# A hybrid mixer's hand-written task order: the second half of the frequencies directly behind the first, first scores between the projection's last steps

## The chip, the cores and the metric

The kernel runs on one core of one Trainium2 chip. Time is device time in microseconds of one launch. The kernel before takes 2418.3 us (median of 3 runs, 2416.39 to 2420.72). All arithmetic is fp32; for the large products an operand is split into a high and a low fp32r part and three products are summed.

## The reference, cut to what matters

Two layers run on 640 tokens (512 latent, 128 context) of width 1024. Each layer is a SwiGLU block, a mixer and a second SwiGLU block, each with modulation by a condition vector. The change lies in the mixer, whose three head groups work on one projection of the same normed input:

```
def mixer(h):                       # per layer, h: 640 x 1024
    u = h @ w_in                    # q, k, v (attention); p (pooling); v0 v1 xa xb xc xd (Hyena)
    pool = group_linear(window_mean(p, 2 | 4 | 8 | 16) - p) * scale
    attn = softmax over |i-j| <= 128 local keys, context keys and a sink (8 heads, 2 kv heads)
    z = (v0, v1)
    for x in ((xa, xb), (xc, xd)):  # Hyena of order 2
        z = short_conv(x) * (long_conv(z) + bias * z)
    return concat(pool, attn, z) @ w_out
```

The long convolution is a transform to frequencies, a product with the filter's spectrum, and the inverse transform, all written as matrix products with tables.

## The kernel before

Channels lie on partitions, tokens on the free axis (640 columns, in two halves of 320). A projection column group of 128 channels is 48 matmuls of 128x320 (8 input channel groups, 3 products of split parts, 2 halves); their PSUM is copied by ScalarE to a tile `u`. The weights come by DMA as `raw`, ScalarE casts them to `whi` (line 294) and VectorE forms `wlo` (line 295).

The mixer's parts are Python generators that issue instructions up to their next `yield`. A string of letters, `MIXP` (line 32), says which generator takes its next step. After it the kernel is compiled by a scheduler which keeps each engine's queue in an order close to this issue order; each engine then works its queue off in order. What follows from the string is thus the order within each queue, and which buffers (rotating slots) are taken over from whom.

The letters that matter here:

- `F` is one step of the projection stream: 12 matmuls, a quarter of the 48 of a column group. The groups come in the order q0 to q3, xa, xb, v, p0, p1, xc, xd; then the output projection's steps. A letter that needs a group which isn't made yet pulls the stream until it is.
- `C` is one step of Hyena (`conv_step_old`, lines 1063 to 1144), for each of its two orders: the transposes `ztp`; the first half of the frequencies (`zf`, then on VectorE `zp`, `zm`, the products `cw`, `cy`, and their sums `pp`, `pmn`); the second half and the context part (`zfc`, `zcs`), with the loads of the four inverse tables `tab` from `in_tfi`; the inverse transform (`yt`, `ytc`); the gate (the short convolution of xc and xd, `sc` with lines 1148 to 1152, the products `yu`, `yw`).
- `P` is the pooling, `pool_mix`: for each of two channel groups the window sums `pw` and the difference `pd` (lines 1171 to 1185, on VectorE, from ScalarE's copies `pl`, `pc`), then in a second step each one's product `pm` and its split `phi`, `plo`.
- `A` is attention: first five steps for head pair 0 (four blocks of scores, each six matmuls `mm<-khi,qhi` and so on and two reductions of line 1398; then the exponentials on ScalarE and the scaling), then the transposes `pt` and products of one pair with the next pair's scores.
- `X` is the context's attention (`sc<-qkc`, `p`), `V` the transposes `vt` of the values, `Q` the queries.

In the stretch that the change re-orders (the second Hyena order), before, the steps come as: first frequency half; pooling group 0; two steps of xc; second frequency half; pooling group 1; inverse transform; the rest of xc; scores block 0; values; block 1; context; block 2; xd, with block 3 and the softmax; the gate (the scheduler takes a block of scores ahead of the inverse transform where it is ready first); the transposes of the probabilities; the output projection.

Of the kernel before, what the change touches and what calls it, by code (L numbers as in the profile page):

```python
# [28 lines left out]
RCP = 300  # L29
RCP2 = 0  # L30
ORDER = "v0 v1 k q0 q1 q2 q3 xa xb v p0 p1 xc xd".split()
MIXP = "FCFFCFFFFFFCFNFCFKFFFFCQQFCQFFQFCPFFCPCFFAVAXAFAAFFCAPFXFAAPFAFFFAFFAAAFAAFFAAFAAAAXFAXFXAFFFFAFABFFBAABBFABAAFAAFFFFFFFF"
PROT = 8
AG0 = (1, 0, 2)
MIXT = 70
# [147 lines left out]
def hybrid_kernel(ctx: ExitStack, tc: tile.TileContext, a, depth=2, fc=22):  # L183
# [974 lines left out]
    def mixer(l, cur, nxt):  # L1158
# [390 lines left out]
        def step(t):  # L1549
            next(tasks[t], None)  # L1550

        for t in MIXP.replace(" ", ""):
            step(t)
# [253 lines left out]
```

## Time and profile before

| | us |
|---|---|
| median of 3 runs | 2418.3 |
| profiled execution | 2417.21 |
| its span in the trace | 2415.4 |
| TensorE busy in the span | 2369.8 (98%) |
| VectorE busy | 1920.3 (80%) |
| ScalarE busy | 1094.6 (45%) |
| mean granted TensorE clock | 0.99 |

The profile is of one execution, and has the durations of all instructions. PE is TensorE, DVE VectorE, ACT ScalarE, SP SyncE, which issues the DMAs. Of a row `out<-in` names the tiles; fp32 matmuls may stand as two records. The time in brackets is the idle time ahead of an instruction, and `<-` what it waited for. The granted clock (PEclk) is 1.00 at the higher of TensorE's two levels and 0.50 at the lower.

### The profile page before, as it was taken

Reading aid. Unit: us, or ns where it says so; the run is one execution under the profiler, and the core shown is the slowest. Engines: PE = TensorE matmul, PEld = TensorE weight load, DVE = VectorE, ACT = ScalarE, POOL = GpSimd, SP = SyncE. Lnnn points to the kernel's source line nnn. Section 1 sums busy time; section 2 is a strip of 40 time slices with the busy share of each in tenths; the row PEclk is TensorE's granted clock in tenths of the full one; section 3 lists DMA queues with packets and bytes.
Section 4 is the critical chain, followed back from the end, with each engine's and each line's share of the span. In section 5 each row is a group of like instructions: output and inputs, shape, how many; then the busy total and the mean of one; then the engine's idle time right before and its main releaser. Section 6 shows DMA issues by size and latency. Waiting matters only on the chain.

```text
span 2415.4 us, 41068 instructions
## 1 busy us (share of the span) xinstructions
PE 2369.8 (98%) x15576; PEld 2246.0 (93%) x15576; DVE 1920.3 (80%) x3885; ACT 1094.6 (45%) x2228; POOL 17.8 (1%) x46
## 2 busy tenths in 40 slices
PE   8999999999989999999999999999998999999999
PEld 3799999999877999999999999999987789999999
DVE  7887888986786798888889889898678678567583
ACT  4653352534345653443535435253434555335251
POOL 0000000000000000000000000000000000000000
PEclk9999999999989999999999999999998999999999
DMA  9434434353210235434343443534231022222222
GB/s 323 168 105 132 134 115 154 101 170 114 102 45 15 78 106 161 127 121 144 117 131 106 124 130 116 164 113 154 89 105 61 18 71 79 79 84 78 85 68 90
DMA packets 132646, 270.37 MB, mean 112 GB/s; under 512 B 15002, under 2 KB 24924, under 8 KB 132320
## 3 DMA queue, kind: packets, MB, share of 16 engines
q1 hardware_dynamic: 132448, 267.75, 34.5%
q8 instruction: 122, 2.00, 0.3%
q14 instruction: 76, 0.62, 0.1%
HBM read 259.56 MB, written 8.13 MB: 111 GB/s over the span
## 4 chain that ended last, share of the span: by engine, by line
PE 93%; DVE 4%; issue 1%; ACT 1%; DMA 1%; SPq 0%; POOL 0%; POOLq 0%; DVEq 0%; ACTq 0%
PE mm L204 79%; PE Z L204 5%; PE yt L204 1%; PE o L204 1%; PE pt L208 1%; PE fk L204 1%; PE mx L204 1%; PE ada L204 1%; PE zf L204 1%; PE rsb L204 0%; PE qbc L204 0%; DMA ar<-in_ada 0%; PE tot L204 0%; DMA par<-in_par 0%; PE nps L204 0%
## 5 line engine op out<-in xcount | busy, mean ns | idle before, releaser
L204 PE MATMUL mm<-hhi,whi 128*128 128x320 f32 x1440 | 448.2, 311 | 1.1 <-ACT u L1220 1.1
L204 PE MATMUL mm<-hlo,whi 128*128 128x320 f32 x1440 | 445.7, 309 | 0.0
L294 ACT CAST whi<-raw 128x512 fp32r<-128x512 f32 (+1 forms) x394 | 238.8, 607 | 456.2 <-PE mm L204 425.9
L204 PE MATMUL mm<-hhi,wlo 128*128 128x320 f32 x1440 | 445.4, 309 | 0.0
L204 PE MATMUL mm<-ahi,whi 128*128 128x320 f32 x1198 | 370.2, 309 | 0.0
L204 PE MATMUL mm<-alo,whi 128*128 128x320 f32 x1198 | 370.2, 309 | 0.0
L204 PE MATMUL mm<-ahi,wlo 128*128 128x320 f32 x1198 | 370.2, 309 | 0.0
L295 DVE TENSOR_TENSOR wlo<-raw,whi 128x512 fp32r<-128x512 f32 (+1 forms) x394 | 262.9, 670 | 77.4 <-ACT whi L294 75.2
L409 DVE CUSTOM_DVE_ANT_0 junk<-araw,condb,par 128x1024 bf16<-128x1024 f32 x240 | 307.1, 1280 | 2.2 <-DMA araw<-in_adat 0.7
L204 PEld LDWEIGHTS mm<-hhi,whi 128*128 128x128 f32 x1440 | 270.3, 188 | 6.0 <-ACT u L1220 2.8
L204 PEld LDWEIGHTS mm<-hlo,whi 128*128 128x128 f32 x1440 | 270.6, 188 | 2.0 <-issue 1.8
L204 PEld LDWEIGHTS mm<-hhi,wlo 128*128 128x128 f32 x1440 | 270.3, 188 | 1.4 <-issue 1.4
L204 PE MATMUL mm<-thi,whi 128*128 128x320 f32 x864 | 267.0, 309 | 0.0
L204 PE MATMUL mm<-tlo,whi 128*128 128x320 f32 x864 | 267.0, 309 | 0.0
L204 PE MATMUL mm<-thi,wlo 128*128 128x320 f32 x864 | 267.0, 309 | 0.0
L204 PEld LDWEIGHTS mm<-ahi,whi 128*128 128x128 f32 x1198 | 224.9, 188 | 0.0
L204 PEld LDWEIGHTS mm<-ahi,wlo 128*128 128x128 f32 x1198 | 224.9, 188 | 0.0
L204 PEld LDWEIGHTS mm<-alo,whi 128*128 128x128 f32 x1198 | 224.9, 188 | 0.0
L294 ACT CAST whi<-ex 128x512 fp32r<-128x512 f32 x216 | 134.2, 621 | 186.9 <-PE mm L204 173.3
L295 DVE TENSOR_TENSOR wlo<-ex,whi 128x512 fp32r<-128x512 f32 x216 | 148.9, 689 | 31.7 <-ACT whi L294 27.2
L294 ACT CAST whi<-ws 128x512 fp32r<-128x512 f32 x144 | 89.4, 621 | 162.2 <-PE mm L204 123.1
L204 PEld LDWEIGHTS mm<-tlo,whi 128*128 128x128 f32 x864 | 162.2, 188 | 0.0
(263 smaller groups left out, 4713.6 us busy)
## 6 DMA issues: line engine op xcount, KB each, us to landing
araw<-in_adat SPq DMA_DIRECT2D x120, 512.0 KB, 3.6
raw<-in_wgu SPq DMA_DIRECT2D x208, 256.0 KB, 3.0
ex<-in_wgu SPq DMA_DIRECT2D x144, 256.0 KB, 2.7
raw<-in_wd SPq DMA_DIRECT2D x128, 256.0 KB, 2.7
raw<-in_win SPq DMA_DIRECT2D x56, 256.0 KB, 2.8
ar<-in_ada SPq DMA_DIRECT2D x48, 256.0 KB, 5.4
raw<-in_wd SPq DMA_DIRECT2D x64, 192.0 KB, 2.6
tab<-in_tfi SPq DMA_DIRECT2D x32, 256.0 KB, 4.1
```

The costliest lines, as they stand in the source:

```text
L204: cls.order(nc.tensor.matmul(**k))
L208: cls.order(nc.tensor.transpose(**k))
L294: S.copy(out=hi, in_=src)
L295: V.tensor_tensor(out=lo, in0=src, in1=hi.bitcast(F32), op=ALU.subtract)
L409: V.tensor_tensor_reduce(out=junk, in0=raw, in1=condb[:, r], scale=1.0, scalar=bias(l, g)[:, s, c, r:r + 1], op0=ALU.mult, op1=ALU.add, ac ...
```

## The change

Only the string `MIXP` is edited; it serves both layers.

```diff
--- before.py
+++ after.py
@@ -29,7 +29,7 @@
 RCP = 300
 RCP2 = 0
 ORDER = "v0 v1 k q0 q1 q2 q3 xa xb v p0 p1 xc xd".split()
-MIXP = "FCFFCFFFFFFCFNFCFKFFFFCQQFCQFFQFCPFFCPCFFAVAXAFAAFFCAPFXFAAPFAFFFAFFAAAFAAFFAAFAAAAXFAXFXAFFFFAFABFFBAABBFABAAFAAFFFFFFFF"
+MIXP = "FCFFCFFFFFFCFNFCFKFFFFCQQFCQFFQFCCPFAFAPAFCAVFAXFFCFAPFXFAAPFAFFFAFFAAAFAAFFAAFAAAAXFAXFXAFFFFAFABFFBAABBFABAAFAAFFFFFFFF"
 PROT = 8
 AG0 = (1, 0, 2)
 MIXT = 70
```

By the steps' names, after the change they come as: first frequency half; second half with the context part; pooling group 0 (with it the projection of p0 and p1); xc step 0; scores block 0; xc step 1; block 1; pooling group 1; block 2; xc step 2; inverse transform; block 3; values; xc step 3; softmax of head pair 0; context; two steps of xd; the gate (with the last two steps of xd); the pooling's products and the first step of the output projection; then transposes and the next pair's scores.

VectorE in layer 0, from the first half's sums `pp`, `pmn` on. Before, a weight split and pooling group 0 (`pw`, `pd`) stand there, and the second half's `zp` inside them:

```order
L1104 TENSOR_TENSOR pp_7300<-cy_7289,cy_7297 128x256 x2
L1105 TENSOR_TENSOR pmn_7301<-cy_7289,cy_7297 128x256 x2
L295 TENSOR_TENSOR wlo_7802<-raw_7799,whi_7801 128x512
L1171 TENSOR_TENSOR pw_7442<-pl_7436 128x527
L295 TENSOR_TENSOR wlo_7914<-raw_7911,whi_7913 128x512
L1181 TENSOR_TENSOR pw_7444<-pw_7442 64x525
L1184 TENSOR_TENSOR pw_7444<-pw_7444,cst 128x8 x2
L1185 SCALAR_TENSOR_TENSOR pd_7438<-pw_7444,cst,u_7368 128x512
L1171 TENSOR_TENSOR pw_7453<-pc_7437 128x143
L295 TENSOR_TENSOR wlo_8023<-raw_8020,whi_8022 128x512
L1181 TENSOR_TENSOR pw_7455<-pw_7453 64x141
L1098 TENSOR_TENSOR zp_7505<-zod_7503,zf_7493 128x512
```

After:

```order
L1104 TENSOR_TENSOR pp_7300<-cy_7289,cy_7297 128x256 x2
L1105 TENSOR_TENSOR pmn_7301<-cy_7289,cy_7297 128x256 x2
L1098 TENSOR_TENSOR zp_7318<-zod_7316,zf_7306 128x512
L1099 SCALAR_TENSOR_TENSOR zm_7319<-zod_7316,zf_7306 128x512
L966 TENSOR_TENSOR cw_7322<-zp_7318,kf_7157 128x512
L968 TENSOR_TENSOR cw_7323<-zp_7318,kf_7157 128x256 x2
L970 TENSOR_TENSOR cy_7327<-cw_7322 128x256
L971 TENSOR_TENSOR cy_7327<-cw_7323 128x256
L966 TENSOR_TENSOR cw_7330<-zm_7319,kf_7159 128x512
L968 TENSOR_TENSOR cw_7331<-zm_7319,kf_7159 128x256 x2
```

The second half's sums and products stand directly behind the first half's; the splits and the pooling have moved behind them.

TensorE in layer 0, at the inverse transform. Before, all of it (`yt`) stands behind the first block of scores (`mm<-khi,qhi`):

```order
L204 MATMUL mm_7650<-klo_6961,qhi_7097 128x384
L204 MATMUL mm_7651<-klo_6961,qhi_7097 128x384
L204 MATMUL mm_7650<-khi_6960,qlo_7098 128x384
L204 MATMUL mm_7651<-khi_6960,qlo_7098 128x384
L204 MATMUL yt_7585<-tab_7531,pp_7300 128x256
L204 MATMUL yt_7585<-tab_7533,pp_7300 128x256
L204 MATMUL yt_7585<-tab_7535,pp_7525 128x256
L204 MATMUL yt_7585<-tab_7537,pp_7525 128x256
L204 MATMUL yt_7585<-tab_7531,pmn_7301 128x256
L204 MATMUL yt_7585<-tab_7533,pmn_7301 128x256
L204 MATMUL yt_7585<-tab_7535,pmn_7526 128x256
L204 MATMUL yt_7585<-tab_7537,pmn_7526 128x256
```

After, the first three `yt` stand at the end of p1's matmuls, ahead of xc (`mm<-hhi,whi`, first of 48) and of all scores; the fourth and the rest stand behind another 54 rows, with three blocks of scores among them:

```order
L204 MATMUL mm_7431<-hhi_6109,wlo_7465 128x320
L204 MATMUL mm_7431<-hhi_6113,whi_7464 128x320
L204 MATMUL mm_7431<-hlo_6114,whi_7464 128x320
L204 MATMUL mm_7431<-hhi_6113,wlo_7465 128x320
L204 MATMUL yt_7641<-tab_7344,pp_7300 128x256
L204 MATMUL yt_7641<-tab_7346,pp_7300 128x256
L204 MATMUL yt_7641<-tab_7348,pp_7338 128x256
L204 MATMUL mm_7520<-hhi_6075,whi_7524 128x320
L204 MATMUL mm_7520<-hlo_6076,whi_7524 128x320
L204 MATMUL mm_7520<-hhi_6075,wlo_7525 128x320
```

The tables are now needed ahead of xc, and the inverse transform is spread over the projection.

VectorE in layer 0 again, with the engines that each instruction waits for, where pooling group 1 begins (`pw<-pl` of 128x527). Before, it stands behind the context's products and waits for ScalarE and GpSimd:

```order
L968 TENSOR_TENSOR cw_7545<-zcs_7542,kf_7160 128x256 [waits DVE_49]
L968 TENSOR_TENSOR cw_7545<-zcs_7542,kf_7160 128x256
L970 TENSOR_TENSOR cy_7549<-cw_7544 128x256 [waits DVE_49]
L971 TENSOR_TENSOR cy_7549<-cw_7545 128x256 [waits DVE_49]
L1171 TENSOR_TENSOR pw_7558<-pl_7552 128x527 [waits Activation_49,Pool_49]
L1181 TENSOR_TENSOR pw_7560<-pw_7558 128x525 [waits DVE_49]
L1181 TENSOR_TENSOR pw_7562<-pw_7560 128x521 [waits DVE_49]
L1181 TENSOR_TENSOR pw_7564<-pw_7562 64x513 [waits DVE_49]
L1184 TENSOR_TENSOR pw_7564<-pw_7564,cst 128x8 [waits DVE_49,Activation_49]
```

After, it stands behind the reductions of scores block 1 (line 1398, ISA):

```order
L1185 SCALAR_TENSOR_TENSOR pd_7497<-pw_7514,cst,u_7427 128x128 [waits DVE_49]
L295 TENSOR_TENSOR wlo_7975<-raw_7972,whi_7974 128x512 [waits DMAHW4_49,PE_49,Activation_49]
L1398 ISA sc_7574,m_7540<-mm_7566,m_6928,par_190 128x512 [waits DVE_49,PE_49]
L1398 ISA m_7540 128x1
L1398 ISA sc_7576,m_7541<-mm_7567,m_6928,par_190 128x512 [waits PE_49]
L1398 ISA m_7541 128x1
L1171 TENSOR_TENSOR pw_7584<-pl_7578 128x527 [waits PE_49,Activation_49,Pool_49]
L1181 TENSOR_TENSOR pw_7586<-pw_7584 128x525 [waits DMAHW1_49,DVE_49,PE_49]
L1181 TENSOR_TENSOR pw_7588<-pw_7586 128x521 [waits DVE_49]
L1181 TENSOR_TENSOR pw_7590<-pw_7588 64x513 [waits DVE_49,PE_49]
L1184 TENSOR_TENSOR pw_7590<-pw_7590,cst 128x8 [waits DVE_49,Activation_49]
L1184 TENSOR_TENSOR pw_7590<-pw_7590,cst 128x8
```

Its place is behind two blocks of scores, and its first instructions now wait for TensorE as well.

## Rows read from the trace of the kernel before

**Rows 1.** The page: busy time, share of the span and instructions of each engine.

```profile
PE 2369.8 (98%) x15576; PEld 2246.0 (93%) x15576; DVE 1920.3 (80%) x3885; ACT 1094.6 (45%) x2228; POOL 17.8 (1%) x46
```

**Rows 2.** TensorE's waits: releaser, total, times, longest (us).

```profile
PE pt L208 <- DVE sc L1353: 7.6, 4, 3.6
...
PE yt L204 <- DMA tab<-in_tfi: 3.5, 2, 3.1
```

**Rows 3.** TensorE's timeline, layer 0: start, us, instruction; in brackets idle time and releaser.

```profile
662.23 0.42 PE L204 MATMUL mm<-hhi,whi 128*128 128x320 f32 x1 [0.57 <-ACT u L1220]
...
677.82 0.34 PE L204 MATMUL mm<-khi,qlo 64*128 64x384 f32 x2
...
681.21 2.04 PE L204 MATMUL yt<-tab,pp 128*128 128x256 f32 x4 [3.05 <-DMA tab<-in_tfi]
...
683.72 2.04 PE L204 MATMUL yt<-tab,pp 128*128 128x256 f32 x4 [0.46 <-DMA tab<-in_tfi]
...
688.50 1.89 PE L204 MATMUL yt<-tab,pp 128*128 128x256 f32 x8
...
690.23 1.89 PE L204 MATMUL yt<-tab,pmn 128*128 128x256 f32 x8
...
709.86 0.78 PE L208 MATMUL pt<-ident,sc 128*128 128x128 f32 x2 [3.58 <-DVE sc L1353]
...
717.31 0.41 PE L204 MATMUL mm<-plo,whi 128*128 128x320 f32 x1
...
731.25 0.31 PE L204 MATMUL mm<-yhi,wlo 128*128 128x320 f32 x1
...
731.40 0.31 PE L204 MATMUL mm<-phi,whi 128*128 128x320 f32 x1
```

**Rows 4.** TensorE's timeline, layer 1: the same two points.

```profile
1817.35 0.42 PE L204 MATMUL mm<-hhi,whi 128*128 128x320 f32 x1 [0.57 <-ACT u L1220]
...
1887.94 0.31 PE L204 MATMUL mm<-phi,whi 128*128 128x320 f32 x1
```

**Rows 5.** Busy time by stretch: us, PE, PEld, DVE, ACT, POOL, PEclk, DMA share, GB/s.

```profile
680.00:690.00 10.00, 8.33 (x27) 6.56 (x28) 9.49 (x24) 2.34 (x6) 0.28 (x4) 0.66 0.42 124
...
706.00:718.00 12.00, 8.35 (x30) 5.58 (x30) 10.94 (x24) 7.67 (x17) 0.00 (x0) 0.72 0.06 22
```

**Rows 6.** VectorE's timeline, layer 0.

```profile
663.03 0.69 DVE L1098 TENSOR_TENSOR zp<-zod,zf 128x512 f32<-128x512 f32 x1 [0.45 <-ACT zod L1096]
...
669.46 0.68 DVE L295 TENSOR_TENSOR wlo<-raw,whi 128x512 fp32r<-128x512 f32 x1
...
675.09 0.69 DVE L1098 TENSOR_TENSOR zp<-zod,zf 128x512 f32<-128x512 f32 x1
...
681.27 0.76 DVE L1105 TENSOR_TENSOR pmn<-cy,cy 128x256 f32<-128x256 f32 x2
...
681.94 0.69 DVE L295 TENSOR_TENSOR wlo<-raw,whi 128x512 fp32r<-128x512 f32 x1
...
684.65 0.71 DVE L1171 TENSOR_TENSOR pw<-pl 128x527 f32<-128x527 f32 x1
...
690.58 0.61 DVE L1398 CUSTOM_DVE_ANT_0 sc<-mm,m,par 128x384 f32<-128x384 f32 x1
```

**Rows 7.** SyncE's queue, layer 0: the four table loads.

```profile
678.48 2.37 SPq L260 DMA_DIRECT2D tab<-in_tfi  x4
```

**Rows 8.** ScalarE's timeline, layer 0.

```profile
701.19 0.62 ACT L1349 ACTIVATE sc<-sc,sm 128x384 f32<-128x384 f32 x1 [1.62 <-DVE sm L1347]
...
704.68 0.43 ACT L1220 COPY u<-mm 128x320 f32<-128x320 f32 x1 [0.27 <-PE mm L204]
...
707.53 0.19 ACT L1349 ACTIVATION_READ_ACCUMULATOR sc<-sc,sm 128x1 f32 x1
```

**Rows 9.** VectorE's timeline, layer 0, behind the softmax.

```profile
708.66 0.72 DVE L1150 SCALAR_TENSOR_TENSOR sc<-u,par,sc 128x511 f32<-128x511 f32 x1
...
718.13 1.00 DVE L1196 SCALAR_TENSOR_TENSOR plo<-pm,par,phi 128x320 fp32r<-128x320 f32 x2
```

## The prediction

> **What bounds the kernel now.** I read the busy shares first: TensorE is busy 98% of the span, VectorE 80% [rows 1], so a new order can pay only where TensorE stands still, and any stretch in which it newly stands still costs its full length. Next I read the table of waits: TensorE's largest wait is for the softmax's scaled probabilities (`pt` behind `sc`), and with it goes the inverse transform's wait for its tables (`yt` behind `tab`) [rows 2]. Both lie in the stretch that the change re-orders. Last I read TensorE's timeline there. In layer 0 it runs from the first matmul of projection p1 behind the forward transform (662.23) to the first matmul of the second output group (731.40), 69.17 us; in layer 1 from 1817.35 to 1887.94, 70.59 us [rows 3, 4]. Program order shows the same 307 TensorE instructions between these two points before and after, in both layers, so the change is the difference in these two stretches.
>
> What TensorE could win there: in layer 0 it waits 3.05 and 0.46 us for tables and 3.58 us for the softmax [rows 3]; besides, its clock stands at the lower level for part of 680 to 690 and of 706 to 718 (mean granted 0.66 and 0.72), each time after it had begun to idle [rows 5]. Summing spacings by kind (0.15 us a 320-column matmul, 0.43 us a 256-column fp32 one, half of the distance 1.73 between 688.50 and 690.23 over two such, and so on [rows 3]) I get about 53.3 us at full clock, so at most 69.2 - 53.3 = 15.9 us are to be won in layer 0 and about 17.3 in layer 1.
>
> **What the change moves.** It adds and removes no arithmetic. It does four things: (1) the second frequency half's products go on VectorE directly behind the first half's; (2) the pooling's first channel group goes behind them, the second one behind two blocks of scores; (3) the first head pair's scores go on TensorE between the last projection steps, ahead of the inverse transform's later parts; (4) the gate's inputs xc and xd, and so their copies on ScalarE, come behind the exponentials.
>
> **Step 1, tables and inverse transform.** VectorE's first half begins at 663.03 and is gap-free up to the weight split at 669.46 [rows 6]. Before, the second half began at 675.09; now it follows at 669.46, 5.63 us earlier, and its last product ends near 669.46 + 6.44 = 675.9 (675.09 to the end of `pmn` at 681.94, less 0.41 us of pooling between). The four table loads wait for this half's first products: before they were issued 678.48 - 675.09 = 3.39 us behind its start [rows 6, 7]; now 2.98, at 672.4. The first `yt` started 2.73 us behind the issue [rows 3, 7], so now at 675.2. But TensorE has less to do until then: 48 matmuls of p1 (7.1 us) and two small fp32 products (0.87) end near 670.2. It waits 5.0 us instead of 3.5: 1.5 us lost. Three `yt`, with the third table as late as before (2.5 us behind the first), end near 677.5; then projection xc and scores block 0 follow.
>
> **Step 2, the wait that is new.** VectorE now does, behind 675.9: two weight splits (1.2), the context's products (2.0), pooling group 0 (3.4), one split (0.6), four score reductions (2 x 0.55 and 2 x 0.68); it ends near 686. Scores block 2 on TensorE needs the score buffers that the reductions of block 1 free, so TensorE stands still again from about 682.5 to 686. Behind it stand, in the same queue, three scores' pairs (0.65), six projection matmuls (0.88), nine `yt` (9 x 0.43) and `ytc` (0.44): 5.9 us, to about 692. The first instruction of pooling group 1 (`pw` from `pl`) now waits for the fourth `yt` matmul of the second channel half, since its output takes over a buffer that this matmul reads, and its next instructions for the `yt` behind it; before it waited for no TensorE work and ran at 684.65 [rows 6]. So VectorE stands still from about 686 to 692, and queued behind the waiting `pw` are the reductions of score blocks 2 and 3 and with them the whole softmax. This is the term on which the forecast rests. No row of before shows this wait; its bounds are 0 (if the buffer comes free in time) and 6.8 us (a lower-clock stretch of TensorE on top); I take 6, from the queue's own sum.
>
> **Step 3, softmax, gate, output.** From 692.1: pooling group 1 takes 690.58 - 684.65 = 5.93 us [rows 6], a split 0.6, reductions of blocks 2 and 3 1.5 and 1.25, small copies 1.2: exponentials begin near 702.6; before they began at 701.19 [rows 8]. Before, ScalarE had copied xd between the exponentials of the two heads (704.68) and the last ended at 707.62 [rows 8]. Now both heads (2 x 2.7), their sinks (0.45), two weight casts (1.1), the context's exponentials (1.4) and the short convolution's scaling (0.8) stand in one row, to about 711.8. Then VectorE does the gate's 17 instructions, 7.6 us by the durations behind 708.66, two `ylo` (1.5) and the `plo`, of which the third ends near 722.5. Before, the `plo` ran partly ahead of `ylo`, and the corresponding output matmul started at 717.31 [rows 3, 9]. TensorE has done its other work by about 711 and stands still until about 721: 9 to 10 us, where before it had 3.58.
>
> **Sum.** From 717.31 to 731.40 TensorE needed 14.1 us [rows 3]. After 722.5 there is the same work and 2.65 us more (six scores and seven transposes of the next head that stood earlier before), and about 1 us at the lower clock: 722.5 + 14.1 + 2.65 + 1 = 740.2, that is +8.8 us in layer 0. Layer 1 repeats the stretch 1155.12 us later; 740.2 + 1155.12 = 1895.3 against 1887.94 [rows 4], +7.4. Together +16 us. The profiled execution took 2417.2, 1.1 below the median of the runs; on the median 2418.3 + 16 = **2434 us**.
>
> **Bounds of the unknown terms.** The table loads: the third `yt` waited to 683.72 [rows 3]; if all tables land as that one, step 1 costs 2 us more a layer. The clock: in rows 5 a mean of 0.66 over 10 us is 6.8 us at the lower level, half speed; if it falls so at each of the three new stops and half of that meets work, I estimate up to 3 us more a layer; if it does not fall, 1 us less. The new wait of VectorE: with 0 in place of 6 the mean of both layers, +8.1, falls to +2.1. So a layer lies between about +2.1 and +13.
>
> **Rivals.**
> A (forecast): VectorE's pooling waits for the inverse transform, softmax and gate come late; +16.
> B: as A, and late tables and the lower clock cost 2 and 3 us a layer more: 2418.3 + 16 + 10 = 2444 us. For it: each stop in rows 5 has such a stretch. Against it: two of the three new stops hide part of theirs in the next stop.
> C, the other side: the order does what its names say. Scores and softmax run under the projection, and the inverse transform starts earlier and leaves the path. It decides at one point: the third `plo` has to be done by 713.6, that is 731.40 - 14.1 - 2.65 - 1; before that the kernel is faster, by what it stays below. For it: the scores stand ahead of the projection's last steps, and the tables are issued 6 us earlier. Against it: the waiting `pw` in front of the softmax. Its price: at the 53.3 us limit plus about 7 of waits for tables, 722.5, -8.9 a layer, 2400 us.
> The Trainium skill has a rule for this, "Perfetto Trace Analysis", section "Optimization Strategy": where the most contended engine changes over time, interleaving the regimes may pay. By it scores between projection steps should fill TensorE's waits; the trace bears the rule's premise out (VectorE and ScalarE are the late engines at 701 to 718, TensorE elsewhere), and by it alone the result would be C.
> D: the earlier tables and the new waits cancel, or the new wait of VectorE is short: 0 to +2.4 a layer, 2418 to 2423.
>
> **How the numbers follow.** Chances: A 0.65, B 0.13, C 0.12, D 0.10. A alone is 2426 to 2440. The range leaves out most of C and the top of B: 2420 to 2444. A measurement of this kernel tells 0.2%, 4.8 us, from no change. Slower by more than that: A, B and a little of D, 0.81. Within it: most of D and the edge of C, 0.09. Faster: 0.10.
>
> **What would show it.** Right: TensorE's first `yt` waits near 5 us for `tab`; VectorE idles about 6 us ahead of a `pw` (line 1171) released by TensorE's `yt`; TensorE idles 8 to 10 us ahead of the first output matmul on `phi` or `plo`, near 711 to 721; the first exponentials of the scores begin no earlier than 701. Wrong: that `pw` starts without a wait, exponentials begin by 696, or the second output group's matmul starts below 731.40 in layer 0.

## The result, and the profile after

The changed kernel takes 2451.1 us (median of 4 runs, 2447.21 to 2454.85) against 2419.5 of the kernel before on the same chip: ratio 1.0132, 95% interval 1.0109 to 1.0154, so **31.6 us slower**. The direction was forecast, the size was not: 2434 was said, and the time lies above the range's 2444. The profiled execution took 2448.4 us, its span 2446.6.

The page's first line, of the kernel after [rows 1 of before]:

```profile
PE 2377.1 (97%) x15576; PEld 2252.3 (92%) x15576; DVE 1922.4 (79%) x3885; ACT 1095.3 (45%) x2228; POOL 18.0 (1%) x46
```

The work is the same; the span is longer by 31.2 us, and TensorE's busy time by 7.3. So TensorE stands still longer, and part of what it does takes longer. Where both lie, a table by stretch shows (us, then the busy time of PE, PEld, DVE, ACT, POOL, the granted clock, DMA). First before, from the first matmul of p1 to the second output group's first matmul, in layers 0 and 1 [rows 3, 4]:

```profile
662.23:731.40 69.17, 62.00 (x346) 50.64 (x346) 59.05 (x161) 33.05 (x87) 0.56 (x8) 0.90 0.15 47
1817.35:1887.94 70.59, 62.62 (x346) 50.89 (x346) 59.15 (x161) 33.20 (x87) 0.63 (x8) 0.90 0.14 46
```

The same two points after:

```profile
662.27:747.52 85.25, 67.59 (x345) 55.13 (x346) 59.90 (x159) 33.19 (x85) 0.56 (x8) 0.82 0.11 38
1833.54:1918.33 84.79, 67.40 (x345) 54.69 (x345) 59.92 (x159) 33.19 (x85) 0.56 (x8) 0.84 0.12 37
```

This is nearly the whole account. The stretch is 16.1 us longer in layer 0 and 14.2 in layer 1. In layer 0 idle time grew from 7.2 to 17.7 us (+10.5), and the same instructions (of the 346 records one is missing after) were busy 67.6 instead of 62.0 us (+5.6), because more of them ran at the lower clock; in layer 1 it is +9.4 and +4.8. All the rest of the span is 0.9 us longer.

What TensorE waited for, after (total, times, longest) [rows 2 of before]:

```profile
PE mm L204 <- ACT phi L1195: 17.9, 2, 9.0
PE yt L204 <- DMA tab<-in_tfi: 9.0, 2, 4.5
PE mm L204 <- DVE m L1398: 7.1, 4, 3.5
```

The softmax's `pt` is gone from the top; in its place the first output matmul waits 9.0 us a layer for the pooling's `phi`, and a block of scores 3.5 us for its buffer. TensorE's timeline in layer 0, after [rows 3]:

```profile
662.27 0.42 PE L204 MATMUL mm<-hhi,whi 128*128 128x320 f32 x1 [0.56 <-ACT u L1220]
...
674.95 2.04 PE L204 MATMUL yt<-tab,pp 128*128 128x256 f32 x4 [4.51 <-DMA tab<-in_tfi]
...
700.63 0.69 PE L204 MATMUL mm<-khi,qhi 64*128 64x384 f32 x1 [3.46 <-DVE m L1398]
...
727.27 0.63 PE L204 MATMUL mm<-phi,whi 128*128 128x320 f32 x1 [8.97 <-ACT phi L1195]
...
747.52 0.42 PE L204 MATMUL mm<-phi,whi 128*128 128x320 f32 x1
```

Three stops, each with a stretch at the lower level behind or inside it; the granted clock is the last number but two (1.00 is the higher of TensorE's two levels) [rows 5 of before]:

```profile
670.00:680.00 10.00, 5.13 (x17) 3.85 (x17) 9.86 (x24) 3.24 (x7) 0.14 (x2) 0.66 0.44 157
...
700.00:710.00 10.00, 9.37 (x32) 7.62 (x33) 6.62 (x25) 6.10 (x17) 0.00 (x0) 0.50 0.09 29
...
720.00:730.00 10.00, 2.73 (x8) 2.08 (x9) 9.39 (x17) 3.13 (x6) 0.00 (x0) 0.52 0.00 0
730.00:740.00 10.00, 10.00 (x58) 8.90 (x58) 4.48 (x13) 3.01 (x11) 0.00 (x0) 0.80 0.09 28
```

From 700 to 710 TensorE is almost fully busy, at half speed throughout: that is where most busy time is lost. VectorE's rows of after [rows 6]:

```profile
669.50 0.68 DVE L1098 TENSOR_TENSOR zp<-zod,zf 128x512 f32<-128x512 f32 x1
...
685.95 0.08 DVE L1398 DVE_READ_ACCUMULATOR2_ANT m<- 128x1 f32 x1
693.38 0.71 DVE L1171 TENSOR_TENSOR pw<-pl 128x527 f32<-128x527 f32 x1 [7.35 <-PE yt L204]
```

The forecast wait is there, in the row forecast: pooling group 1 stands 7.35 us behind the inverse transform. ScalarE's rows of after [rows 8]:

```profile
692.42 0.62 ACT L1168 COPY pl<-u 128x512 f32<-128x512 f32 x1 [8.46 <-PE yt L204]
...
705.54 0.61 ACT L1349 ACTIVATE sc<-sc,sm 128x384 f32<-128x384 f32 x1 [1.95 <-DVE sm L1347]
...
711.89 0.62 ACT L294 CAST whi<-raw 128x512 fp32r<-128x512 f32 x1 [3.35 <-PE mm L204]
712.42 0.61 ACT L1349 ACTIVATE sc<-sc,sm 128x384 f32<-128x384 f32 x1
...
726.06 0.72 ACT L294 CAST yhi<-yw 128x640 fp32r<-128x640 f32 x1 [0.93 <-DVE yw L1141]
726.69 1.78 ACT L1195 ACTIVATE phi<-pm,par 128x320 fp32r<-128x320 f32 x4
```

Here is what was not forecast. The copy `pl`, which `pw` reads, waits for a `yt` matmul too, 8.46 us, and ends at 693.04, only 0.34 us before `pw` starts: the pooling's wait stands in two queues. The second head's exponentials start at 712.42, behind a weight cast that waits 3.35 us until TensorE's matmuls (at the lower clock) free its buffer. And `phi`, whose input `pm` was done by 718.3, stands behind both casts of the gate's output `yhi`.

### The profile page after: what moved, and what is told of

Same layout as the page of the kernel before. It is cut to its first block, busy times and chain, and to the rows that moved or that the text cites. A ratio compares the mean times of both kernels' runs of the same rounds, so it can differ in the third digit from the quotient of the medians.

```text
span 2446.6 us, 41080 instructions
## 1 busy us (share of the span) xinstructions
PE 2377.1 (97%) x15576; PEld 2252.3 (92%) x15576; DVE 1922.4 (79%) x3885; ACT 1095.3 (45%) x2228; POOL 18.0 (1%) x46
## 5 line engine op out<-in xcount | busy, mean ns | idle before, releaser
L204 PEld LDWEIGHTS mm<-thi,wlo 128*128 128x128 f32 x864 | 162.2, 188 | 0.0
L204 PEld LDWEIGHTS mm<-thi,whi 128*128 128x128 f32 x864 | 162.2, 188 | 0.0
```

The costliest lines, as they stand in the source:

```text
L204: cls.order(nc.tensor.matmul(**k))
```

## The experiments

Only the piece of `MIXP` behind the common start `...FFQFC` is edited unless said otherwise. The piece of the kernel before is `PFFCPCFFAVAXAFAAFFC APFX...`, of the changed kernel `CPFAFAPAFCAVFAXFFCF APFX...`. Ratios are to the kernel before on the same chip, with 95% intervals; "us" is the ratio less one, times 2418.3, which puts the change itself at +31.9. Theory T: the scores ahead of pooling and softmax make the loss. Rival R: the early frequencies and their wait for tables make it.

| run | median us | ratio (interval) | us |
|---|---|---|---|
| e1_freq | 2419.1 | 1.0001 (0.9990 to 1.0013) | +0.2 |
| e2_scores | 2446.0 | 1.0118 (1.0103 to 1.0134) | +28.5 |
| e3_pool | 2430.4 | 1.0060 (1.0036 to 1.0083) | +14.5 |
| e4_back | 2435.1 | 1.0073 (1.0058 to 1.0088) | +17.7 |
| e5_cast | 2445.7 | 1.0109 (1.0095 to 1.0124) | +26.4 |
| e6_pm | 2442.2 | 1.0102 (1.0086 to 1.0118) | +24.7 |
| e7_near | 2426.1 | 1.0033 (1.0021 to 1.0045) | +8.0 |
| e8_far | 2422.2 | 1.0014 (1.0004 to 1.0024) | +3.4 |
| f1_fill_tab | 2450.5 | 1.0126 (1.0113 to 1.0140) | +30.5 |
| f2_fill_both | 2440.4 | 1.0096 (1.0080 to 1.0113) | +23.2 |
| f3_before_fill | 2416.5 | 0.9981 (0.9970 to 0.9993) | -4.6 |
| f4_before_fill2 | 2418.7 | 0.9996 (0.9985 to 1.0008) | -1.0 |
| h1_all | 2420.4 | 1.0007 (0.9996 to 1.0018) | +1.7 |
| h2_all_fill | 2417.9 | 0.9999 (0.9989 to 1.0009) | -0.2 |
| h3_freq_fill | 2414.4 | 0.9984 (0.9973 to 0.9995) | -3.9 |

**The two halves of the change.**

```diff
 e1_freq, against the kernel before
-PFFCPCFFAVAXAFAAFFC
+CPFFPCFFAVAXAFAAFFC
 e2_scores, against the changed kernel
-CPFAFAPAFCAVFAXFFCF
+PFFCAFAPACAVFAXFFCF
```

> The kernel before with one step of the order moved: the second half of the frequencies directly behind the first; pooling and scores stay as before. Theory T (the loss comes from pooling group 1 and the softmax standing behind the inverse transform): TensorE waits about 5 us for the tables instead of 3.5, scores keep their place, so 0 to +4 us on the kernel before. Rival R (the early frequency half and the wait for tables with the low clock behind it make the loss): +12 to +30 us.

> The other part alone: the second half of the frequencies stays two projection steps behind pooling group 0 as before; scores block 0 and 1 stand between the projection's steps, pooling group 1 behind them and the rest as in the changed kernel. Theory T: most of the loss, +22 to +34 us on the kernel before, with VectorE again idle ahead of pooling group 1 or TensorE idle 8 us or more ahead of the first output matmul. Rival R: under +10 us.

The frequency half alone costs nothing that can be told, the other half (the early scores, with pooling group 1 behind them) nearly everything; R falls. Yet e1_freq has the longer wait for tables, in its table of waits:

```profile
PE yt L204 <- DMA tab<-in_tfi: 9.5, 3, 4.4
PE pt L208 <- DVE sc L1353: 7.2, 4, 3.4
```

The tables' wait is 2.7 times that of before [rows 2], 6 us more, and most of that comes back: the two stretches of this trace are 70.49 and 71.41 us, 2.1 us more than before together. The wait for the softmax behind it stays (7.2 against 7.6 us), which suggests that the softmax ends last there in both kernels.

**Pooling group 1 ahead of its wait.** Two ways, against the changed kernel:

```diff
 e3_pool
-CPFAFAPAFCAVFAXFFCF
+CPPFAFAAFCAVFAXFFCF
 e4_back
-CPFAFAPAFCAVFAXFFCF
+CPCFAFAPAFAVFAXFFCF
```

> The changed kernel with one letter moved: pooling group 1 directly behind group 0, ahead of the scores; the program then has no wait of its first instruction for TensorE. Theory T: VectorE's 7 us of idle time ahead of it go, the first exponentials come some 5 to 7 us earlier, and of the +32 us about 10 to 18 go: +13 to +22 us on the kernel before. Rival R: the tables are as late and the inverse transform as split as in the changed kernel: +26 to +34 us.

> The changed kernel with the inverse transform's step ahead of the first scores, so that it is not split by scores and projection steps and pooling group 1, where it stays, finds its buffers free. Theory T: VectorE doesn't wait for TensorE there, exponentials 4 to 6 us earlier: +14 to +24 us on the kernel before. Rival R in the form that the split of the inverse transform is what costs: 0 to +8 us.

Both times came as T said, and R's versions of both failed. In e3_pool the group runs without the wait (VectorE, ScalarE, TensorE):

```profile
680.87 0.70 DVE L1171 TENSOR_TENSOR pw<-pl 128x527 f32<-128x527 f32 x1
```

```profile
696.72 0.62 ACT L1349 ACTIVATE sc<-sc,sm 128x384 f32<-128x384 f32 x1
...
714.77 1.77 ACT L1195 ACTIVATE phi<-pm,par 128x320 fp32r<-128x320 f32 x4
```

```profile
715.34 0.64 PE L204 MATMUL mm<-phi,whi 128*128 128x320 f32 x1 [8.51 <-ACT phi L1195]
```

The stretch begins at 660.07 in this execution, at 662.27 in the changed kernel's. Counted from there, the first exponentials start 6.6 us earlier than in the changed kernel and 2.3 us earlier than before the change [rows 3, 8], and still the kernel is 14.5 us slower than before: it waits 8.5 us for `phi`. So about 17 us (12 to 23 by the interval of this run's ratio) were the pooling's wait, and the rest lies behind the softmax.

In e4_back the exponentials start 3.1 us earlier, counted in the same way, less than the 4 to 6 expected. The wait ahead of `pw` is gone, but VectorE now waits for TensorE at the first scores instead:

```profile
688.18 0.62 DVE L1398 CUSTOM_DVE_ANT_0 sc<-mm,m,par 128x384 f32<-128x384 f32 x1 [5.07 <-PE mm L204]
```

**The cast and the pooling's products.** Against the changed kernel:

```diff
 e5_cast
-CPFAFAPAFCAVFAXFFCF APFXFAAPF...
+CPFAFAPAFCAVAFXFFCF APFXFAAPF...
 e6_pm
-CPFAFAPAFCAVFAXFFCF APFXFAAPF...
+CPFAFAPAFCAVFAXFFPPCF AFXFAAF...
```

> The changed kernel with one letter moved: the softmax step of the first head pair one projection step earlier, so that on ScalarE a weight cast, which waits for TensorE to free its buffer, stands behind the second head's exponentials instead of ahead of them. Theory: that cast held the exponentials back by 3.4 us a layer, which the prediction had priced at the cast's own 0.6; moved, 3 to 8 us go of the change's +32 (about 2443 to 2448 us). Rival: the chain behind is held by something else (pooling, gate), and nothing goes: 2449 to 2453.

> The changed kernel with the pooling's products pm, phi and plo asked for ahead of the gate instead of behind it. Theory: the first output matmul then waits for the gate's yhi and ylo alone, the 9.0 us of waiting for phi become 2 to 5 us for yhi, and of the +32 us 4 to 9 go (2442 to 2447). Rival: the gate is what ends last, the output matmul waits as long for yhi, 2449 to 2453.

Both as the theories had it: 5.5 and 7.2 us go. In e5_cast the cast that waits for TensorE has moved behind the second head (ScalarE):

```profile
704.72 0.61 ACT L1349 ACTIVATE sc<-sc,sm 128x384 f32<-128x384 f32 x1 [0.72 <-DVE sm L1347]
...
709.99 0.61 ACT L1349 ACTIVATE sc<-sc,sm 128x384 f32<-128x384 f32 x1
711.52 0.62 ACT L294 CAST whi<-raw 128x512 fp32r<-128x512 f32 x1 [0.73 <-PE mm L204]
```

In e6_pm the wait of 9.0 us for `phi` is one of 2.8 for `yhi` (TensorE):

```profile
723.42 0.63 PE L204 MATMUL mm<-yhi,whi 128*128 128x320 f32 x2 [2.83 <-ACT yhi L294]
725.05 0.63 PE L204 MATMUL mm<-ylo,whi 128*128 128x320 f32 x1 [1.01 <-DVE ylo L295]
```

**The three moves together.**

```diff
 h1_all, against the changed kernel
-CPFAFAPAFCAVFAXFFCF APFXFAAPF...
+CPPFAFAAFCAVAFXFFPPCF AFXFAAF...
```

> The changed kernel with the three moves of the runs before together: pooling group 1 ahead of the scores, the first softmax one projection step earlier, the pooling's products ahead of the gate. Theory (they are three separate terms of the loss): 20 + 5 + 9 us of the +32 go, 2414 to 2422 us, level with the kernel before. Rival (they shorten one chain, and the early scores still cost something of their own): 2424 to 2432.

The three moves together bring the kernel back to where it was: the theory held. With them the early scores cost nothing that can be measured, and gain nothing. By the ratios the single runs give 17.4 + 5.5 + 7.2 = 30.1 us and this one 30.2; with intervals of 3 to 6 us to either side, that they agree so well is luck. The stretches tell more. Of e3_pool, e5_cast, e6_pm and h1_all, two layers each:

```profile
660.07:735.42 75.35, 61.76 (x346) 51.16 (x346) 59.66 (x159) 33.08 (x85) 0.56 (x8) 0.89 0.13 42
1820.89:1896.00 75.11, 61.52 (x346) 50.93 (x346) 59.64 (x159) 32.97 (x85) 0.56 (x8) 0.89 0.13 43
661.61:744.26 82.65, 68.06 (x346) 56.38 (x346) 59.99 (x159) 33.20 (x85) 0.56 (x8) 0.83 0.11 38
1829.84:1911.82 81.98, 67.40 (x346) 55.22 (x346) 60.00 (x159) 33.20 (x85) 0.56 (x8) 0.83 0.12 39
658.76:738.88 80.12, 67.69 (x345) 55.32 (x345) 59.48 (x159) 32.95 (x85) 0.56 (x8) 0.85 0.12 40
1826.32:1906.20 79.88, 67.96 (x345) 55.50 (x345) 59.46 (x159) 32.95 (x85) 0.56 (x8) 0.85 0.12 40
663.33:733.39 70.06, 61.00 (x345) 50.87 (x345) 59.09 (x159) 32.99 (x85) 0.56 (x8) 0.90 0.13 45
1820.42:1890.46 70.04, 61.03 (x346) 50.85 (x346) 59.06 (x159) 32.98 (x85) 0.56 (x8) 0.90 0.14 45
```

Both layers together take 170.0 us in the changed kernel and 139.8 before. The single moves take off 19.6, 5.4 and 10.0 us, 35.0 in all; the three together take off 29.9. So, by one execution of each, some 5 us are counted twice: the moves are not quite separate terms, they shorten in part the same chain.

**The clock.** Matmuls that compute nothing new stand where TensorE waits; the next real matmul overwrites them.

```diff
 f1_fill_tab and f2_fill_both (5, on the changed kernel), f3_before_fill (3, rhs=zm, on the kernel before), h2_all_fill (5, on h1_all), h3_freq_fill (5, on e1_freq)
             ps = mix(512, "yt")
+            if o == 1 and c == 0:
+                for _ in range(5):
+                    PE.matmul(out=ps, lhsT=ident, rhs=pq[0][0].rearrange("p a b -> p (a b)"), start=True, stop=True)
 ...
 f2_fill_both too, ahead of the first output group (9)
+                for _ in range(9 if n == 0 else 0):
+                    PE.matmul(out=ps[0], lhsT=ident, rhs=x[:, 7, 0:512], start=True, stop=True)
 ...
 f4_before_fill2: f3_before_fill and ahead of head 0's first transposes (3)
+                    if j == 0 and kb == 0 and kv == 0:
+                        for _ in range(3):
+                            PE.matmul(out=ps, lhsT=ident, rhs=x[:, 7, 0:512], start=True, stop=True)
```

> The changed kernel with five fp32 matmuls of 512 columns (about 0.87 us each at full clock, their result overwritten by the inverse transform's first matmul) in TensorE's queue where it waits 4.5 us for the tables, in the second Hyena order of both layers: the wait is worked through, so the lower clock behind it should not come. Theory (a third of the loss is the clock, which falls behind each new stop): the stretch of 6.8 us at the lower clock near 673 goes, the work in it runs at full speed, and 1 to 4 us go (2447 to 2450 us), less than that work's 4 us in two layers where VectorE is late anyway. Rival (the clock does not matter, only the chain of waits): within 1 us of 2451.

> As the run before, and nine such matmuls where TensorE waits 9.0 us for phi ahead of the first output matmul. Theory: the output steps behind that wait run at full clock: 727 to 734 us took 7.1 us at the lower clock, so some 3 us a layer more go, together 6 to 12 us below the changed kernel (2439 to 2445). Rival: within 1 us of the changed kernel, or slower by what the filling work overruns the wait.

> The kernel before with three such matmuls ahead of the inverse transform, where it waits 3.05 us for the tables. Theory: the lower clock from 680 to 687 does not come, the transform runs at full speed there; but VectorE's pooling covers part of it: -2 to -7 us. Rival: no change within 1.5 us, since scores and softmax behind wait for VectorE.

> As the run before, with three more ahead of the transposes of the probabilities, where TensorE waits 3.58 us for the softmax. Theory: both stretches at the lower clock go: -4 to -12 us. Rival: as the run before or slower.

f1_fill_tab: the lower stretch at the tables is gone, but the runs do not decide between theory and rival: the median is 0.6 us, the ratio 1.4 us below the change, with intervals that overlap. The trace speaks for a small gain. Its two stretches are 2.0 and 1.6 us shorter than the changed kernel's:

```profile
668.30:751.58 83.28, 69.20 (x355) 54.80 (x355) 59.74 (x159) 33.08 (x85) 0.56 (x8) 0.88 0.11 38
1837.13:1920.33 83.20, 69.44 (x355) 54.91 (x355) 59.82 (x159) 33.09 (x85) 0.56 (x8) 0.88 0.12 39
```

In layer 0 only 0.6 us of this is there at the stop ahead of scores block 3, which is as long as in the changed kernel (3.45 us): VectorE is late behind the tables. f2_fill_both: the theory held, 8.7 us less than the change, and the mean clock of layer 0's stretch is 0.94 (busy time now holds the filling):

```profile
661.20:741.91 80.71, 74.73 (x373) 56.56 (x373) 59.74 (x159) 33.11 (x85) 0.57 (x8) 0.94 0.12 39
```

So the filling ahead of the output steps, and with it the clock behind that last wait, is worth some 7 us of the 32 (8.7 less f1's 1.4 by the ratios; 6.6 by the stretches). The rows show where: from the first output matmul to the second group's first one layer 0 takes 16.3 us here and 20.3 in the changed kernel. It is not a term to be added to those of h1_all, which shorten the same wait. The stop ahead of scores block 3 was filled in no run. On the kernel before the three fillings at the tables win 4.6 us. Three more at the transposes win nothing more: they also changed the order around those transposes, and layer 0 fell to the lower clock (0.73 from 720 to 725, 0.59 from 725 to 730) where layer 1 did not, so this run decides nothing on that second wait.

> As the run before, with five filling matmuls where TensorE waits for the tables. Theory: the lower clock of 6.8 us behind that wait goes; where TensorE is the late engine behind it, 2 to 6 us less than the run before; rival: within 1.5 us of it, as in the changed kernel with the same filling, where VectorE was late.

> The frequency half alone moved, which was level with the kernel before, and five filling matmuls in its wait for the tables. Theory: TensorE works at full speed through the inverse transform, as in the kernel before with filling (-4.5 us): 2412 to 2416. Rival: the tables' longer wait is what counts, 2417 to 2421.

h2_all_fill is 1.9 us below h1_all by the ratios, with intervals that overlap, and its stretches (69.52 and 69.58 us) are 0.5 us shorter each: between theory and rival. h3_freq_fill is as the theory said, 3.9 us faster than the kernel before. It and f3_before_fill beat both kernels (2414.4 and 2416.5 us, not told apart).

**Two that failed.** Two orders found by reasoning on the waits alone, against the kernel before:

```diff
 e7_near
-PFFCPCFFAVAXAFAAFFC APFX...
+FFCPPCFFAVAXAFAAFFC APFX...
 e8_far
+FFCPPCFFVAAXAFAFAFC APAAFXFFPFFAAFAFFAAAAFFFAAFAAAA...
```

> The part of the change that cost nothing, carried on: second frequency half directly behind the first, then both pooling groups, then the inverse transform whole, and only then the projection xc, with the scores inside it; gate and the rest as in the kernel before. Theory: the pooling and the inverse transform are done before the scores, the softmax is released earlier and no engine waits for it: -5 to -12 us on the kernel before. Rival: the tables' wait (4.5 us) and the low clock behind it eat the gain as in the run with the frequency half alone: within 3 us of the kernel before.

> As the run before it in this set, with the values ahead of the scores and the gate, pooling products and first head's transposes spread further among the projection and output steps. Theory: 1 to 4 us below that run. Rival: the same as that run, since the waits left there are the tables' and the end of the mixer's.

Both were slower than before. In e7_near that went against theory and rival. e8_far was to be 1 to 4 us below e7_near and is 4.6 below it by the ratios, 3.9 by the medians; but with e7_near itself 8.0 us slower than before, that wins nothing. In e7_near TensorE waits 4.7 us for `plo` at the output, in e8_far 3.9 us for a score buffer (one row of each):

```profile
718.42 0.63 PE L204 MATMUL mm<-plo,whi 128*128 128x320 f32 x1 [4.74 <-DVE plo L1196]
```

```profile
718.46 1.33 PE L204 MATMUL mm<-khi,qhi 64*128 64x512 f32 x2 [3.89 <-DVE m L1398]
```

A reading that no run tests: the early inverse transform took work from TensorE that before stood behind it, and what it then waited for came no earlier. Which of the moved letters did it was not tried.

## Why the prediction was wrong

- **Place and signs: right.** All but 0.9 us of the 31.2 lie in the two stretches named, and the four signs named for being right came: the waits for `tab`, ahead of `pw` and ahead of the first output matmul (8.97 us, 8 to 10 said, but up to 727.3 and not 721), and exponentials no earlier than 701. The bounds were not right: a layer was to lie between +2.1 and +13, and the two are +16.1 and +14.2.
- **Step 1: right.** Tables were issued at 672.08 (672.4 said), the first `yt` started at 674.95 (675.2), after 4.51 us of waiting (5.0). e1_freq shows that this step by itself costs too little to be told.
- **Step 2: right in mechanism, a little short.** The wait of `pw` is 7.35 us (6 said, 6.8 the upper bound) and ends at 693.38 (692.1). That its input `pl` waits as well was not seen. The stop said for 682.5 to 686 did not come: TensorE reached scores block 1 only at 683.38, partly because of the lower clock (0.57 from 676 to 680), and five projection matmuls ran ahead of block 2. e3_pool puts the whole step at 17.4 us for both layers.
- **Step 3: mis-sized, and this is the step that failed.** Exponentials start at 705.54, not 702.6: 1.3 us come from step 2, the rest is that scores block 3 waited 3.46 us for its buffer and then ran at half speed. The row of ScalarE's work put at 711.8 ends at 718.2, 3.5 us later still: "two weight casts (1.1)" were priced at their length, but one stands in an in-order queue and waits 3.35 us for TensorE. e5_cast moves that cast and gets 5.5 us back for both layers. Third `plo` near 729.0 (727.56 and three of four 0.48) instead of 722.5. Of the 7.3 us by which layer 0 missed (747.52 against 740.2) 6.5 stand at this point, 5.2 of them from step 3 itself; the last 0.8 lie behind it, where the granted clock is 0.50 up to 731.
- **The clock: taken at 1 us more a layer, bounded at 3; busy time grew by 5.6 and 4.8.** By the rows it acts through step 3: of the matmuls that stand ahead of the waiting cast, those up to 710 ran at half speed. No run filled the stop ahead of them, so what the clock adds to that wait is read from rows and not shown by an experiment; f2_fill_both shows it for the output steps. The sum counted stops of TensorE and a chain on VectorE and ScalarE apart; in the rows they feed each other.
- **Rivals.** B had the right ingredient in the clock; the tables were not late (the third `yt` starts at 677.35, after another 0.35 us), and even its 2444 was short. C did not come about: with the three moves of h1_all the early scores leave the kernel level with the old order, 1.0007. The Trainium skill ("Perfetto Trace Analysis", section "Optimization Strategy") says that interleaving regimes may improve performance where the most contended engine changes over time. No run here shows a gain by the early scores.

## What to carry to other kernels

When a step moves ahead of another, look on every engine's queue for what now stands in front of the late chain: here a pooling step, a weight cast and a gate, of three different tasks, gave back 17.4, 5.5 and 7.2 us when they were moved out of the way, and what the early scores cost without these waits is not told from nothing (h1_all: 1.7 us, interval -1.0 to 4.4). A cast or copy that refills a buffer is as long as the wait for the buffer's last reader, not as long as its own row: 3.35 us of waiting for a cast of 0.62. And a new stop of TensorE can be dearer than its length where the work behind it is what others wait for: here 9.4 us of work ran at half speed behind a stop of 3.46 us.

## What was not expected of the hardware

Filling a wait of TensorE with matmuls kept the granted clock at the higher level (0.82 to 0.94 over layer 0's stretch in f2_fill_both) and made the kernel before faster by 4.6 us (0.9981, 0.9970 to 0.9993) with more work in it. What the filling at the tables' wait is worth seems to depend on the order around it. By the stretches of both layers, of one execution each, it takes 4.1 us off the kernel before, 4.1 off e1_freq, 3.6 off the changed kernel and 1.0 off h1_all. The two layers of one execution differ by as much as 1.4 us (69.17 and 70.59 before), so the last is not told from nothing. Why it differs, no run shows.
